# A byte offset for one operand of the combined column tiles

## The chip, the cores and the metric

The kernel runs on one core of one Trainium2 chip. The metric is the device time of one execution in microseconds. The kernel before takes 2104.44 us, the median of three runs (2104.36 to 2105.59).

## What is computed

One decoder block on a sequence of 512 tokens of width 2048, in float32. The part that matters here is the second half, the gated feed-forward:

```
h = rms_norm(x, norm2) * (1 + sc2) + sh2
gate, val = split(h @ w_up)            # w_up: 2048 x 12288
gate = causal_dwconv(gate, ffn_conv_w, ffn_conv_b)
x = x + g2 * ((gelu(gate) * val) @ w_down)
return rms_norm(x, norm_final)
```

Before it come the conditioning (`c` through `w_ada`), the input projection, two mixers and the output projection.

## The kernel before

Activations lie transposed, 128 features by 512 tokens to a tile. A float32 matrix product is made of products of rounded parts: a weight tile `raw` (128 x 1024) is rounded by ScalarE into `wh` (`round_up`, L163), and VectorE writes what was cut off, `raw - wh`, into `wl` (`rest`, L168), the weights' rest. Activations have such a pair too, `hi` and `lo`.

The program is a list of 516 steps, one weight tile each. A step has its tile rounded and its rest written two steps ahead (`round_step`, `rest_step` in the main loop), so that `wh` and `wl` have three buffers each, in a pool of their own at the low end of SBUF.

The stages are: 96 steps of input and output projections, 16 steps for the first four columns of `w_up` (`PLAIN`), 308 steps of combined columns, and 96 steps of `w_down`. Plain steps use `mm_w` or `mm_h`: per weight slice of 128 columns three matmuls of 512 columns, `wh` with `hi`, `wh` with `lo` and `wl` with `hi` (L174 to L176; `mm_h`, L181 to L183, has the roles of weights and activations exchanged).

A combined column is one of the other 44 columns of 128 gate and 128 value features. It is made of seven products of sums of weight blocks with sums of activation blocks (`P1` to `P7`, `product`), each one step. Such a step does eight times the same pair of matmuls:

```
PE.matmul(both, hi[:, cs], m, start=first, stop=False, skip_group_check=True)
PE.matmul(ps[:, lower], lo[:, cs], m[:, 0, :], start=False, stop=last, skip_group_check=True)
```

The first (L921) has 128 columns of `wh` as the stationary operand and 512 moving columns, the `hi` and `lo` parts of 256 tokens; the second (L922) has the same 128 columns of the rest `wl` and 256 moving columns. Each needs its own weight load. In these steps the weight tile is not fetched by `fetch` but named by `source[j]`: a tile `rawb`, `raw` or `t` that DMAs and VectorE have summed (`column`). `source` therefore holds just the 308 combined steps.

The order of instructions is the order in which the main loop issues them (`manual_schedule`); no planner moves them.

In the built program `wh` begins at bytes 1152, 5248 and 9344 of a partition and `wl` at 13440, 17536 and 21632. All matmul operands of the combined steps begin at a multiple of 64 bytes, and at the same remainder by 512.

Of the kernel before, what the change touches and what calls it, by code (L numbers as in the profile page):

```python
# [10 lines left out]
F32R = mybir.dt.float32r  # L11
# [4 lines left out]
P = 128  # L16
S = 512
# [14 lines left out]
NMM = 6  # L32
NXS = 24
WBUFS = 3


ROUNDS = [(0, 2), (2, 6), (6, 10), (10, 16)]
# [13 lines left out]
def tile_block(ctx, tc, x_t, vec, w_ada, w_in, w_r, w_i, ws_t, w_out, w_up, w_us, w_dn, out):  # L51
# [3 lines left out]
    wts = ctx.enter_context(tc.tile_pool(name="weights", bufs=1))  # L55
# [5 lines left out]
    def sb(tag, bufs, shape=(P, S), dt=F32, pl=pool):  # L61
        count[0] += 1
        return pl.tile(list(shape), dt, name=f"{tag}_{count[0]}", tag=tag, bufs=bufs)
# [97 lines left out]
    def round_up(raw):  # L161
        hi = sb("wh", WBUFS, (P, 2, S), F32R, wts)
        A.copy(hi, raw)  # L163
        return hi

    def rest(raw, hi):
        lo = sb("wl", WBUFS, (P, 2, S), F32R, wts)
        V.tensor_tensor(out=lo, in0=raw, in1=hi, op=SUB)  # L168
        return [(hi[:, kk, :], lo[:, kk, :]) for kk in range(2)]

# [90 lines left out]
    raws, his, ws, source = {}, {}, {}, {}  # L261
# [12 lines left out]

    def rest_step(j):
        if j < len(steps):
            ws[j] = rest(raws.pop(j), his.pop(j))

    def group(srcs, ks, op, rhs, done, small=0):

# [250 lines left out]
    round_step(0)  # L531
    next(cgen)
    rest_step(0)
    settle_h()
    round_step(1)
    fetch(3, SY)
    need(1)
    rest_step(1)
    fetch(4, SY)

# [623 lines left out]
    for f in range(FT):  # L1164
        if f < EARLY + 26:
            j = J1 + f // 2
# [6 lines left out]
    for k in range(KT):  # L1173
        j = place["P1", PLAIN + 2 + 5 * k // 2]
# [31 lines left out]
    for j, (_, go, done) in enumerate(steps):  # L1206
# [5 lines left out]
        if j == UP0:  # L1212
            rest_step(j + 1)
# [85 lines left out]
```

## Time and profile before

| what | value |
| --- | --- |
| median of three runs | 2104.44 us |
| profiled execution, device time | 2104.92 us |
| its span, first to last instruction | 2103.2 us |
| TensorE busy | 2069.0 us (98%) |
| VectorE busy | 1492.9 us (71%) |
| ScalarE busy | 923.8 us (44%) |
| combined columns, first to last matmul | 688.78 to 1559.26 us of the span |
| mean granted clock of TensorE | 0.993 of full speed |

The page gives the busy share of each engine, then the chain of work that ended last, then groups of instructions. A matmul's start is measured and its end is modelled, so that back-to-back matmuls overlap in the record; the distance from one start to the next tells what a matmul takes in a stream.

### The profile page before, as it was taken

The page shows a single profiled execution, that of the slowest core. Times are in us where ns is not written, and L with a number is a line of the kernel's source. Part 1 is how long each engine was busy: PE and PEld are TensorE (multiplying, and loading weights), DVE is VectorE, ACT ScalarE, POOL GpSimd, SP SyncE. Part 2 cuts the span into 40 slices and gives each one's busy share as a digit, 9 for nine tenths or more (in the row PEclk, how much of TensorE's full clock was granted, in tenths as well). Part 3 has the DMA queues.
Part 4 walks back from the last instruction along what each step waited for, and adds up shares of the span by engine and source line. Part 5 has one row for each costly group of instructions (what it writes and reads, how often), then busy time and mean ns, then how long its engine had stood idle before and what let it go on. Part 6 is the DMA issues. An engine that isn't in the chain of part 4 may idle for free.

```text
span 2103.2 us, 26309 instructions
## 1 busy us (share of the span) xinstructions
PE 2069.0 (98%) x10160; PEld 1727.6 (82%) x10160; DVE 1492.9 (71%) x1865; ACT 923.8 (44%) x1165; POOL 79.7 (4%) x100
## 2 busy tenths in 40 slices
PE   7999999999989999999999999999999999999997
PEld 4887777888868888888888888888888888888886
DVE  8999889788767888888888888888875223432333
ACT  5323666332234555555555555555553222322223
POOL 0000000000000000000000000000000000000000
PEclk9999999999999999999999999999999999999999
DMA  9977434589825677877877867767755334423222
GB/s 374 327 288 264 141 127 154 199 296 367 298 95 159 212 225 202 241 216 202 242 216 204 240 211 210 248 198 235 216 177 199 121 119 141 159 91 99 92 90 100
DMA packets 116061, 420.36 MB, mean 200 GB/s; under 512 B 14816, under 2 KB 14944, under 8 KB 103648
## 3 DMA queue, kind: packets, MB, share of 16 engines
q1 hardware_dynamic: 87280, 315.39, 42.6%
q0 software_dynamic: 12672, 46.14, 11.6%
q10 hardware_dynamic: 15984, 57.15, 7.9%
q8 instruction: 80, 1.31, 0.2%
q14 instruction: 45, 0.37, 0.0%
HBM read 397.66 MB, written 20.97 MB: 199 GB/s over the span
## 4 chain that ended last, share of the span: by engine, by line
PE 87%; DVE 7%; ACT 3%; issue 1%; DMA 1%; SPq 0%; ACTq 0%; DVEq 0%
PE mm L921 28%; PE mm L922 14%; PE mm L174 13%; PE mm L175 13%; PE mm L176 13%; DVE araw L212 2%; PE mm L181 1%; PE mm L183 1%; PE mm L182 1%; DVE wl L168 1%; DMA araw<-w_ada 1%; DVE xs L359 1%; PE sm L655 0%; DVE la L685 0%; DVE xs L734 0%
## 5 line engine op out<-in xcount | busy, mean ns | idle before, releaser
L163 ACT CAST wh<-raw 128x1024 fp32r<-128x1024 f32 x296 | 311.7, 1053 | 615.1 <-PE mm L175 443.1
L168 DVE TENSOR_TENSOR wl<-raw,wh 128x1024 fp32r<-128x1024 f32 x296 | 360.9, 1219 | 303.8 <-ACT wh L163 303.4
L921 PE MATMUL mm<-hp,wh 128*128 128x512 f32 x1408 | 499.5, 399 | 0.0
L174 PE MATMUL mm<-hp,wh 128*128 128x512 f32 x1184 | 469.0, 396 | 6.7 <-ACT hp L229 5.8
L175 PE MATMUL mm<-hp,wh 128*128 128x512 f32 x1184 | 463.6, 392 | 0.5 <-DVE hp L237 0.5
L176 PE MATMUL mm<-hp,wl 128*128 128x512 f32 x1184 | 462.8, 391 | 0.0
L922 PE MATMUL mm<-hp,wl 128*128 128x256 f32 x1408 | 395.4, 281 | 0.0
L921 PE MATMUL mm<-xs,wh 128*128 128x512 f32 x1056 | 375.1, 399 | 0.0
L921 PEld LDWEIGHTS mm<-hp,wh 128*128 128x128 f32 x1408 | 264.6, 188 | 66.1
L922 PE MATMUL mm<-xs,wl 128*128 128x256 f32 x1056 | 296.6, 281 | 0.0
L174 PEld LDWEIGHTS mm<-hp,wh 128*128 128x128 f32 x1184 | 223.7, 189 | 58.3 <-ACT hp L229 8.7
L922 PEld LDWEIGHTS mm<-hp,wl 128*128 128x128 f32 x1408 | 266.0, 189 | 0.0
L175 PEld LDWEIGHTS mm<-hp,wh 128*128 128x128 f32 x1184 | 223.6, 189 | 50.1 <-issue 2.4
L176 PEld LDWEIGHTS mm<-hp,wl 128*128 128x128 f32 x1184 | 223.6, 189 | 46.6
L168 DVE TENSOR_TENSOR wl<-rawb,wh 128x1024 fp32r<-128x1024 f32 x176 | 214.9, 1221 | 65.6 <-ACT wh L163 65.6
L921 PEld LDWEIGHTS mm<-xs,wh 128*128 128x128 f32 x1056 | 198.4, 188 | 49.6
L922 PEld LDWEIGHTS mm<-xs,wl 128*128 128x128 f32 x1056 | 199.5, 189 | 0.0
L163 ACT CAST wh<-rawb 128x1024 fp32r<-128x1024 f32 x176 | 185.2, 1052 | 23.9 <-PE mm L921 13.3
L212 DVE SCALAR_TENSOR_TENSOR araw<-araw,crow 128x2050 f32<-128x2050 f32 (+1 forms) x80 | 182.6, 2286 | 2.5 <-DMA araw<-w_ada 2.4
L950 POOL DMA_DIRECT2D raw<-w_us x88 | 75.9, 862 | 1240.8 <-DMA rawb<-w_us 457.8
L974 ACT COPY u<-mm 128x512 f32<-128x512 f32 x88 | 51.7, 587 | 161.5 <-PE mm L922 161.5
L168 DVE TENSOR_TENSOR wl<-t,wh 128x1024 fp32r<-128x1024 f32 x44 | 53.9, 1225 | 50.3 <-ACT wh L163 50.3
(233 smaller groups left out, 2106.3 us busy)
## 6 DMA issues: line engine op xcount, KB each, us to landing
rawb<-w_us SPq DMA_DIRECT2D x132, 512.0 KB, 6.8
araw<-w_ada SPq DMA_DIRECT2D x48, 1024.5 KB, 7.6
raw<-w_dn SPq DMA_DIRECT2D x96, 512.0 KB, 3.6
raw<-w_us SPq DMA_DIRECT2D x88, 512.0 KB, 6.2
raw<-w_us POOLq DMA_DIRECT2D x88, 512.0 KB, 7.3
araw<-w_ada SPq DMA_DIRECT2D x32, 1025.0 KB, 8.4
raw<-w_in ACTq DMA_DIRECT2D x59, 512.0 KB, 4.6
yl<-w_ada SPq DMA_DIRECT2D x16, 1024.5 KB, 5.4
```

The source lines that it names most:

```text
L163: A.copy(hi, raw)
L168: V.tensor_tensor(out=lo, in0=raw, in1=hi, op=SUB)
L174: PE.matmul(ps, w[0][:, cs], h[0], start=first, stop=False)
L175: PE.matmul(ps, w[0][:, cs], h[1], start=False, stop=False)
L176: return PE.matmul(ps, w[1][:, cs], h[0], start=False, stop=last)
L181: PE.matmul(ps, h[0][:, cs], w[0], start=first, stop=False)
L182: PE.matmul(ps, h[0][:, cs], w[1], start=False, stop=False)
L212: V.scalar_tensor_tensor(out=raw, in0=raw, scalar=1.0, in1=crow[:, :w], op0=MUL, op1=MUL, accum_out=mods[:, n:n + 1])
L921: PE.matmul(both, hi[:, cs], m, start=first, stop=False, skip_group_check=True)
L922: PE.matmul(ps[:, lower], lo[:, cs], m[:, 0, :], start=False, stop=last, skip_group_check=True)
L950: G.dma_start(o[name], w_us[f - PLAIN, i], accum_op=ADD)
L974: A.copy(t, o["x"])
```

## The change

`wl` buffers grow from 1024 to 1088 float32 per partition, 4096 to 4352 bytes. In the 308 combined steps the rest is written to, and read from, elements 8 to 1031 of its buffer, in all other steps from elements 0 to 1023.

```diff
+OFFSET = 8
...
-    def rest(raw, hi):
-        lo = sb("wl", WBUFS, (P, 2, S), F32R, wts)
+    def rest(raw, hi, off=0):
+        whole = sb("wl", WBUFS, (P, 2 * S + 64), F32R, wts)
+        lo = whole[:, off:off + 2 * S].rearrange("p (a b) -> p a b", a=2)
         V.tensor_tensor(out=lo, in0=raw, in1=hi, op=SUB)
...
-            ws[j] = rest(raws.pop(j), his.pop(j))
+            ws[j] = rest(raws.pop(j), his.pop(j), OFFSET if j in source else 0)
```

On all five engines the instructions, their order and their waits are row for row the same. What differs is where tiles lie: `wl` begins at bytes 13440, 17792 and 22144, and 32 more in the combined steps, and what stands above it in the lower part of SBUF (`yl`, `fy`, `rawb`, `dp`, `t2`, `gw`, `vw` and others) moves up by 768 bytes. `wh`, `hp`, `xs` and `raw` stay.

## Rows read from the trace of the kernel before

**Rows 1.** Page, part 1 (busy us, share, instructions) and part 4 (chain, by engine).

```profile
PE 2069.0 (98%) x10160; PEld 1727.6 (82%) x10160; DVE 1492.9 (71%) x1865; ACT 923.8 (44%) x1165; POOL 79.7 (4%) x100
...
PE 87%; DVE 7%; ACT 3%; issue 1%; DMA 1%; SPq 0%; ACTq 0%; DVEq 0%
```

**Rows 2.** Busy time in one stretch of the combined columns, with granted clock.

```profile
core 0: us, PE busy (x) PEld busy (x) DVE busy (x) ACT busy (x) POOL busy (x), PEclk, DMA share, GB/s
700.00:1569.60 869.60, 869.60 (x4911) 753.60 (x4910) 720.27 (x781) 477.84 (x575) 72.29 (x84) 1.00 0.74 219
```

**Rows 3.** Page, part 5: the second matmul of a pair, by moving tile.

```profile
L922 PE MATMUL mm<-hp,wl 128*128 128x256 f32 x1408 | 395.4, 281 | 0.0
...
L922 PE MATMUL mm<-xs,wl 128*128 128x256 f32 x1056 | 296.6, 281 | 0.0
```

**Rows 4.** Timeline, TensorE, into the combined columns: start us, modelled length, instruction.

```profile
688.55 0.39 PE L176 MATMUL mm<-hp,wl 128*128 128x512 f32 x1
688.78 0.39 PE L921 MATMUL mm<-hp,wh 128*128 128x512 f32 x1
689.00 0.28 PE L922 MATMUL mm<-hp,wl 128*128 128x256 f32 x1
689.12 0.40 PE L921 MATMUL mm<-hp,wh 128*128 128x512 f32 x1
689.35 0.28 PE L922 MATMUL mm<-hp,wl 128*128 128x256 f32 x1
689.47 0.40 PE L921 MATMUL mm<-hp,wh 128*128 128x512 f32 x1
689.71 0.28 PE L922 MATMUL mm<-hp,wl 128*128 128x256 f32 x1
689.83 0.40 PE L921 MATMUL mm<-hp,wh 128*128 128x512 f32 x1
```

**Rows 5.** Timeline, TensorE, out of the combined columns into `w_down`.

```profile
1559.26 0.28 PE L922 MATMUL mm<-hp,wl 128*128 128x256 f32 x1
1559.38 0.40 PE L174 MATMUL mm<-xs,wh 128*128 128x512 f32 x1
...
1560.31 0.39 PE L175 MATMUL mm<-xs,wh 128*128 128x512 f32 x1
```

**Rows 6.** Timeline, TensorE, in `w_down`: eleven plain matmuls, first and last.

```profile
1619.69 0.39 PE L176 MATMUL mm<-dp,wl 128*128 128x512 f32 x1
...
1621.96 0.39 PE L174 MATMUL mm<-dp,wh 128*128 128x512 f32 x1
```

**Rows 7.** Timeline, matmuls (PE) and weight loads (PEld) of one pair.

```profile
1200.04 0.40 PE L921 MATMUL mm<-hp,wh 128*128 128x512 f32 x1
1200.04 0.19 PEld L922 LDWEIGHTS mm<-hp,wl 128*128 128x128 f32 x1
...
1200.27 0.28 PE L922 MATMUL mm<-hp,wl 128*128 128x256 f32 x1
1200.27 0.19 PEld L921 LDWEIGHTS mm<-hp,wh 128*128 128x128 f32 x1
```

**Rows 8.** Weight loads elsewhere: a timeline row, then two lines' min/median/max ns.

```profile
592.56 0.97 PEld L136 LDWEIGHTS sm<-ones,sqs 128*128 128x128 f32 x8 [2.72 <-issue]
...
L515 PEld LDWEIGHTS sm<-xs,ones x16: 186/190/191, 10.3 to 17.4; 128*128 128x128 f32 x16
...
L655 PEld LDWEIGHTS sm<-la,wi x16: 186/190/190, 203.3 to 317.8; 128*128 128x128 f32 x16
```

**Rows 9.** VectorE's writes: duration min/median/max ns, first and last start.

```profile
L168 DVE TENSOR_TENSOR wl<-rawb,wh x176: 1210/1220/1226, 679.0 to 1554.2; 128x1024 fp32r<-128x1024 f32 x176
...
L212 DVE SCALAR_TENSOR_TENSOR araw<-araw,crow x80: 2262/2286/2296, 18.5 to 570.9; 128x2049 f32<-128x2049 f32 x48, 128x2050 f32<-128x2050 f32 x32
```

## The prediction

> **What bounds the kernel.** The page comes first. TensorE is busy for 98% of the span and holds 87% of the chain of work that ended last [rows 1]. Then comes the stage that the change touches, the combined columns. [...]
>
> The number of pairs is the count of L922, 1408 with a moving tile `hp` and 1056 with `xs`, in sum 2464 [rows 3]. The pitch comes from the timeline: the first L921 starts at 688.78 [rows 4], the last L922 at 1559.26 [rows 5]. That is 870.48 us for 2463 whole pairs and one step from L921 to L922 (0.24), so 870.24 / 2463 = 0.3533 us a pair. The reader should see how even this is: in [rows 4] the pairs after the first begin at 689.12, 689.47 and 689.83, so 0.35 and 0.36 apart, and the stage as a whole has the same mean.
>
> Is 0.3533 all that the matmuls need? Two rows say that it is a little more. In a plain stream of 512-column matmuls, each with a weight load of its own, ten steps take 1621.96 - 1619.69 = 2.27 us, 0.227 each [rows 6]. The first pair of the stage, which comes after such a stream, takes 689.12 - 688.78 = 0.34: 0.22 to 0.23 for the 512 columns and 0.11 to 0.12 for the 256. From the second pair on the 512-column step takes 0.23 to 0.24 [rows 4]. And when the stage ends, four 512-column matmuls in `w_down` take 1560.31 - 1559.38 = 0.93, 0.2325 each, before that stream runs at 0.227 too [rows 5, 6]. So in the pairs something costs 0.3533 - 0.34 = 0.0133 us each, and it needs some matmuls to die away. What differs from a plain stream is that weight loads come more densely: one begins with every matmul [rows 7], and a matmul of 256 columns is over in 0.12 while eight loads behind one another, with matmuls of one column, take 0.97 us, some (0.97 - 0.19) / 7 = 0.111 each [rows 8]. Loads nearly fill the short matmul and reach into the long one. That much the rows bear out; whether the disturbance has to do with the byte at which an operand begins they don't show, since before the change all operands of the pair begin at the same remainder by 512 bytes.
>
> **The change part by part.** It removes and adds no instruction, moves none and adds no wait. Four things remain to be costed.
>
> First, the 2464 loads of a rest, which now begin 32 bytes past a multiple of 64. This is the term on which all hangs, and no row shows it directly. The nearest is a load of `ones`, a tile that lies 32 bytes past a multiple of 64 in the kernel before: L515 loads it 16 times, in 186 to 191 ns, and L655 loads gate weights, which begin at a multiple of 64, in 186 to 190 ns [rows 8]. The load itself thus takes the same. These matmuls are unrounded float32 ones, though, in which the load has much more room, so that the row bounds the load and not a conflict of the load with the stream beside it. From both sides: at best the disturbance is gone and every pair takes the 0.34 of the first, 2464 x -0.0133 = -32.8 us; at worst every pair takes the 0.36 that now one in three shows, 2464 x (0.36 - 0.3533) = +16.5 us. I take 0, by [rows 8], for a second reason too: the load of a rest runs beside the long matmul, 0.23 us [rows 7] for a load that alone needs 0.111. The load in the tight place, beside the 256 columns, is that of `wh`, and `wh` isn't moved.
>
> [...]
>
> Second, the 308 writes of a rest by VectorE at the new start. Now a write takes 1220 ns [rows 9]. The nearest row is L212, which works in place on two buffers of 8200 bytes, 8224 apart: every other one begins 32 bytes past a multiple of 64. All 80 take 2262 to 2296 ns [rows 9], with no second level among them. So 0, and a cover stands behind it: VectorE is idle for 869.60 - 720.27 = 149.3 us of the stage [rows 2], 0.49 us for each of some 307 writes, so that a write must become 40% longer before VectorE is what the stage waits for. A rest is written two steps, 16 pairs, ahead of its use in the program's order.
>
> Third, the 208 plain rests, two thirds of them in buffers that begin 256 or 512 bytes further on. Their stream takes 0.227 with moving tiles that lie in quite different places, `hp`, `xs` and `dp` among them, so 0.
>
> Fourth, the tiles above that move by 768 bytes. That is a multiple of 64 and of 256, none of them is a weight, and only `dp` is a moving operand. 0.
>
> The sum is 0 against the profiled 2104.92 us, of which 2103.2 are the span and 1.7 lie around it. The median of the runs is 0.5 lower, and I forecast that median: 2104.4.
>
> **The rivals.** *Faster: the shift parts the load of the rest from the stream beside it.* If the disturbance comes from load and stream reading at the same remainder of an address, the shift takes the rest's half of it away. Then the long step goes back to the 0.227 of a plain stream and the short one stays at the 0.12 of [rows 4]: 0.347 a pair, 2464 x (0.347 - 0.3533) = -15.5 us, 2088.9. For it speaks that the excess is there and lies in the long step, in which the rest is loaded. Against it: that step may be long only because the load of `wh`, begun beside the 256 columns, isn't done when it starts, and this one keeps its place. A whole recovery, 2071.6, would need both.
>
> *Slower: the shift puts the load of the rest in the stream's way.* The place is the same step, from L921 to L922. If a start that isn't a multiple of 64 costs the load an extra read, or moves it into the slots of the 512 moving columns, each pair goes to the slow 0.36: +16.5 us, 2120.9. A load that only takes longer decides nothing until it exceeds 0.227, twice its 0.111; one that takes slots from the stream costs from the first pair on. Against it stands the equal load of `ones`.
>
> *The change doesn't do what it says.* Only steps in `source` get the offset, and these are all 308 products, each with one write and eight loads; the built program has the offset on all of them. No chance is kept for this.
>
> **How the numbers follow.** Nothing changes: 0.60. Faster by the recovery: 0.22, since the excess is in the rows and depends on how loads and streams meet. Slower by a new conflict: 0.18, since with equal ignorance of addresses the shift may do harm as well as good, but has less room by the row of `ones`. A partial effect is as likely as a full one, so that the two prices are spread from the edge of "the same" to their ends. A measurement tells 0.2% from no change here, 4.2 us. The range takes in no change, recoveries down to 2090 and losses up to 2114, some three fifths of the price; it leaves out about 0.15. The chances are 0.22 faster, 0.60 within 0.2%, 0.18 slower.
>
> **What would show it.** If I am right, the pair's pitch in the combined columns is 0.3533 after as before, with the same steps of 0.23 to 0.24 and 0.12, the stage lasts 870.5 us, writes of the rest stay at 1220 ns and TensorE is still busy for the whole of it. The faster rival shows as a long step of 0.227 and a stage of some 855 us; the slower one as a pair of 0.36 and some 887 us. A write of the rest well above 1.22 us with TensorE waiting for it would break the second step; a plain stream off 0.227 would break the third or the fourth.

## The result and the profile after

The changed kernel takes 2089.44 us, the median of four runs (2087.23 to 2090.37), against 2104.89 us before, the median of four runs on the same occasion. The ratio is 0.9923, with a 95% interval from 0.9911 to 0.9936: 15.5 us faster, where no change was forecast.

The profiled execution took 2090.37 us with a span of 2088.6 us, 14.6 us less than before. Page, part 1, which answers to [rows 1]:

```profile
PE 2053.3 (98%) x10160; PEld 1720.6 (82%) x10160; DVE 1493.7 (72%) x1865; ACT 919.8 (44%) x1165; POOL 81.3 (4%) x100
```

TensorE's busy time fell by 15.7 us with the same 10160 matmuls; VectorE's rose by 0.8. Timeline of TensorE, from the first pair of the combined columns to the last, with eight steps out of the middle (start us, modelled length, instruction); L924 and L925 are the lines that were L921 and L922:

```profile
690.14 0.40 PE L924 MATMUL mm<-hp,wh 128*128 128x512 f32 x1
...
1200.44 0.40 PE L924 MATMUL mm<-xs,wh 128*128 128x512 f32 x1
1200.68 0.28 PE L925 MATMUL mm<-xs,wl 128*128 128x256 f32 x1
1200.80 0.39 PE L924 MATMUL mm<-xs,wh 128*128 128x512 f32 x1
1201.02 0.28 PE L925 MATMUL mm<-xs,wl 128*128 128x256 f32 x1
1201.13 0.40 PE L924 MATMUL mm<-xs,wh 128*128 128x512 f32 x1
1201.37 0.28 PE L925 MATMUL mm<-xs,wl 128*128 128x256 f32 x1
1201.49 0.39 PE L924 MATMUL mm<-xs,wh 128*128 128x512 f32 x1
1201.71 0.28 PE L925 MATMUL mm<-xs,wl 128*128 128x256 f32 x1
...
1544.22 0.28 PE L925 MATMUL mm<-hp,wl 128*128 128x256 f32 x1
```

The stage lasts 1544.22 - 690.14 = 854.08 us instead of 870.48 [rows 4, 5]. That is 16.40 us less; the stage began 1.36 us later than before and what follows it took 0.44 longer, which together give the span's 14.6. A pair now takes (854.08 - 0.23) / 2463 = 0.3467 us instead of 0.3533. The eight steps show how: every second pair is a fast one of 0.22 + 0.11 (1200.80 to 1201.13), the one behind it takes 0.24 + 0.12. In the trace the two pitches are 340 and 353 to 354 ns in turn, from the sixth pair to the end of the stage; the first five take 349 to 352. Before, the 340 stood only at the very start [rows 4]; from there on the pairs took 350, 361 and 349 ns in turn, a cycle of three.

Busy time in nearly all of the stage, which answers to [rows 2]: TensorE still never waits (844.00 us busy of 844.00, before 869.60 of 869.60), and its granted clock is 1.00 as before.

```profile
700.00:1544.00 844.00, 844.00 (x4872) 739.09 (x4871) 712.86 (x771) 468.22 (x569) 72.29 (x84) 1.00 0.75 222
```

VectorE's write of the rest (L171, before L168) and a plain stream of eleven matmuls in `w_down`, which answer to [rows 9] and [rows 6]:

```profile
L171 DVE TENSOR_TENSOR wl<-rawb,wh x176: 1210/1220/1228, 680.4 to 1539.4; 128x1024 fp32r<-128x1024 f32 x176
```

```profile
1605.79 0.39 PE L178 MATMUL mm<-dp,wh 128*128 128x512 f32 x1
...
1608.05 0.39 PE L179 MATMUL mm<-dp,wl 128*128 128x512 f32 x1
```

The write takes 1220 ns as before, and ten plain steps take 2.26 us, 0.226 each, as before. So all of the gain is the pitch of the pair.

### The profile page after: what moved, and what is told of

Read it like the earlier page. It is cut to its first block, busy times and chain, and to the rows that moved or that the text cites. A ratio compares the mean times of both kernels' runs of the same rounds, so it can differ in the third digit from the quotient of the medians.

```text
span 2088.6 us, 26309 instructions
## 1 busy us (share of the span) xinstructions
PE 2053.3 (98%) x10160; PEld 1720.6 (82%) x10160; DVE 1493.7 (72%) x1865; ACT 919.8 (44%) x1165; POOL 81.3 (4%) x100
## 4 chain that ended last, share of the span: by engine, by line
PE 87%; DVE 7%; ACT 3%; issue 1%; DMA 1%; SPq 0%; ACTq 0%; DVEq 0%
PE mm L924 27%; PE mm L925 14%; PE mm L177 13%; PE mm L178 13%; PE mm L179 13%; DVE araw L215 2%; PE mm L184 1%; PE mm L186 1%; PE mm L185 1%; DVE wl L171 1%; DMA araw<-w_ada 1%; DVE xs L362 1%; PE sm L658 0%; DVE la L688 0%; DVE xs L737 0%
## 5 line engine op out<-in xcount | busy, mean ns | idle before, releaser
L171 DVE TENSOR_TENSOR wl<-raw,wh 128x1024 fp32r<-128x1024 f32 x296 | 362.0, 1223 | 303.9 <-ACT wh L165 303.5
L924 PE MATMUL mm<-hp,wh 128*128 128x512 f32 x1408 | 490.3, 394 | 0.0
L925 PE MATMUL mm<-hp,wl 128*128 128x256 f32 x1408 | 391.3, 278 | 0.0
L924 PE MATMUL mm<-xs,wh 128*128 128x512 f32 x1056 | 368.2, 394 | 0.0
L924 PEld LDWEIGHTS mm<-hp,wh 128*128 128x128 f32 x1408 | 264.2, 188 | 60.7
L925 PE MATMUL mm<-xs,wl 128*128 128x256 f32 x1056 | 293.4, 278 | 0.0
L925 PEld LDWEIGHTS mm<-hp,wl 128*128 128x128 f32 x1408 | 264.4, 188 | 0.0
L171 DVE TENSOR_TENSOR wl<-rawb,wh 128x1024 fp32r<-128x1024 f32 x176 | 215.0, 1221 | 57.9 <-ACT wh L165 57.9
L924 PEld LDWEIGHTS mm<-xs,wh 128*128 128x128 f32 x1056 | 198.1, 188 | 45.5
L925 PEld LDWEIGHTS mm<-xs,wl 128*128 128x128 f32 x1056 | 198.3, 188 | 0.0
L171 DVE TENSOR_TENSOR wl<-t,wh 128x1024 fp32r<-128x1024 f32 x44 | 53.9, 1225 | 50.5 <-ACT wh L165 50.5
```

## The experiments

What the runs had to tell apart: whether the 32 bytes did it or the new places of the longer buffers; whether a start of its own counts (within 64 bytes) or a distance between two operands; if a distance, that of a load from the moving stream or of the two loads from each other; and whether the distance is all that counts.

All pitches below are from one start of the first matmul of a pair to the next. Where they are given in ns, they are worked out from the starts in the trace; in the table they are means over the last 50 pairs of a block of seven steps. A time without an interval is that of one run. Edits are against the changed kernel, but for the three kernels that shift activations, which start from the kernel before.

### The longer buffers without the 32 bytes

```diff
-OFFSET = 8
+def offsets(j):
+    return 0, 0
...
-            ws[j] = rest(raws.pop(j), his.pop(j), OFFSET if j in source else 0)
+            ws[j] = rest(raws.pop(j), his.pop(j), offsets(j)[1])
```

> The longer rest buffers stay, the 32 bytes go: every rest starts at the beginning of its buffer. If the 32 bytes are the cause, the pitch of a pair in the combined columns is back at 0.3533 us and the time at 2104.9 us. If it is the new places of the buffers (256 and 512 bytes further on) or of the tiles above them, the pitch stays at 0.3467 us and the time at 2089.4 us.

2104.43 us against 2104.24, ratio 1.0004 (0.9995 to 1.0014). First matmuls of a pair in 700 us of the combined columns (busy us of TensorE, count in brackets), before and here:

```profile
800.00:1500.00 700.00, 700.00 (x1982) 372.29 (x1982) 1.00 0.75 222
```

```profile
800.00:1500.00 700.00, 700.00 (x1982) 372.26 (x1982) 1.00 0.75 222
```

In the changed kernel the same 700 us hold 2021:

```profile
800.00:1500.00 700.00, 700.00 (x2021) 378.90 (x2020) 1.00 0.76 224
```

So it is the 32 bytes. That two of the three buffers begin 256 and 512 bytes further on, and the tiles above 768, did nothing.

### Sweeps of the start

Two kernels give each block of seven combined steps an offset of its own.

```diff
+LIST = (0, 1, 2, 3, 4, 5, 6, 7, 8, 10, 12, 14, 16, 18, 20, 24, 28, 32, 40, 48, 56, 64)
...
-            ws[j] = rest(raws.pop(j), his.pop(j), OFFSET if j in source else 0)
+            ws[j] = rest(raws.pop(j), his.pop(j), offsets(j)[1])
```

> The start of the rest differs by combined column: 0, 1, 2, 3, 4, 5, 6, 7, 8, 10, 12, 14, 16, 18, 20, 24, 28, 32, 40, 48, 56, 64 elements (4 bytes each), seven steps with each, and all of them once more; in the last 96 steps four steps with each. If what counts is that the start is not a multiple of 64 bytes (16 elements), pairs take 0.3467 us at every offset but 0, 16, 32, 48 and 64. [...] If it is the distance between two streams, the pitch rises and falls smoothly with the offset, and with no return at 16. Plain matmuls in the last steps stay at 0.227 us at every offset if their loads are hidden.

> The same 22 offsets, given in the first 22 combined columns to the rounded weights alone, the rests at 0; in the other 22 to both alike. Theory one, a load conflicts with the moving stream beside it when both start at the same remainder: shifting both frees both loads, so that the pitch at 8 elements is at most 0.3467 us, perhaps 0.340. Theory two, the two loads that follow one another get in each other's way when they start at the same remainder: shifting the rounded weights alone by 8 gives 0.3467 us as shifting the rests does, and shifting both alike brings 0.3533 us back.

The second kernel has `round_up` take `offsets(j)[0]` in the same way. Each of the two took 2105.84 us. Some of the pitches, in ns, by offset in elements of 4 bytes:

| offset | rest alone, first and second pass | `wh` alone | both alike |
| --- | --- | --- | --- |
| 0 | 353.2, 346.7 | 353.2 | 346.7 |
| 1 | 346.7, 346.7 | 346.6 | 350.0 |
| 2 | 351.1, 351.1 | 346.6 | 346.7 |
| 3 | 356.7, 356.7 | 353.2 | 349.9 |
| 4 | 353.3, 353.3 | 350.0 | 346.7 |
| 8 | 346.7, 346.7 | 351.2 | 353.3 |
| 12 | 346.7, 346.7 | 349.3 | 346.7 |
| 16 | 346.7, 346.7 | 340.0 | 353.3 |
| 24 | 351.7, 351.7 | 350.0 | 346.7 |
| 56 | 353.3, 353.3 | 346.7 | 346.7 |
| 64 | 346.7, 346.7 | 346.7 | 353.2 |

No expectation held as a whole. The pitch isn't a matter of multiples of 64 bytes (4 and 56, which are none, take 353.3; 16 and 64, which are, take 346.7), and it doesn't rise and fall smoothly (346.7 at 1, 356.7 at 3, 346.7 again at 8, 351.7 at 24). Theory one fails as it was stated, since shifting both by 8 is no better than shifting none. Theory two had one thing right, the 353.3 with both shifted by 8, but fails: `wh` alone by 8 doesn't give what the rest alone gives, and with both alike the distance between the two loads stays while the pitch still changes, to 350.0 at 1 and 349.9 at 3. What the table does show: a move of a single element can change the pitch (351.1 at 2, 356.7 at 3 and 353.3 at 4, rest alone, in both passes); all offsets but 0 give the same in both passes, while 0 gives two values; and one entry, `wh` alone by 16 elements, stands at 340.0. In the sweep each entry of the last two columns was met once, behind the offset before it, so that it holds for that way of entering alone.

Plain matmuls weren't indifferent either. In `w_down`, with four steps to an offset of the rest, they took 227.1 ns at 0 and 226.7 at 7, but 229 to 234 at the other offsets short of 64, and 227.5 at 64 (256 bytes). `wh` shifted alone by less than 64 gave 230 to 234. For plain streams the starts of the kernel before are about the best of those tried.

### The activations shifted, by padding

```diff
-        return sb("hp", 16, (P, 2, S), dt)
+        whole = sb("hp", 16, (P, 2 * S + 16), dt)
+        return whole[:, 8:8 + 2 * S].rearrange("p (a b) -> p a b", a=2)
```

> The kernel before, but the pairs of activations (hp) start 32 bytes further on; weights stay. Of the seven products of a column, those with hp as the moving tile then have load and stream at different remainders, those with xs as before. Theory one (load against stream): the pairs with hp take 0.3467 us or less, those with xs 0.3533 us. Theory two (load against load): 0.3533 us everywhere.

2114.8 us. The padding of 64 bytes did more than the expectation says: from one of the 16 buffers to the next 64 bytes more are added up, so that they stand at four different distances from the weights by the remainder of 256 bytes. Plain matmuls with `hp` took 234 ns, pairs with `hp` 349.3 and with `xs`, which weren't moved, 346.8. That the latter changed too says that one pair acts on later ones, so that the comparison within the run doesn't tell the two theories apart; the 346.8 at starts that didn't move is close to the second pitch, 346.7, that offset 0 has in the table. The two runs that follow shift all buffers alike.

### All operands shifted, and the stream alone

A tile of 32 bytes at the low end of the weights' pool, and one at the high end of the main pool, move whole pools.

```diff
     wts = ctx.enter_context(tc.tile_pool(name="weights", bufs=1))
+    wts.tile([P, 8], F32, name="ahead")
...
+    pool.tile([P, 56], F32, name="behind")
     own.__exit__(None, None, None)
```

> Weights, rests and activations all lie 32 bytes further on by the remainder of 256, so that every distance between two operands of a pair stays and only their own remainders change. If distances count, a plain matmul takes 0.227 us and a pair 0.3533 us, 2104.9 us in all. If an operand's own start within 64 bytes counts, plain matmuls take 0.231 us or more, as in the sweep with the weights alone off, and the time rises by some 20 to 30 us.

2106.22 us, one run beside 2104.42. The count in the same 700 us:

```profile
800.00:1500.00 700.00, 700.00 (x1982) 372.23 (x1982) 1.00 0.75 221
```

Every block has 353.2 to 353.4 ns, and plain matmuls with `hp` take 0.227, six in 1.36 us:

```profile
1649.77 0.39 PE L175 MATMUL mm<-hp,wh 128*128 128x512 f32 x1
...
1651.13 0.39 PE L175 MATMUL mm<-hp,wh 128*128 128x512 f32 x1
```

With all distances kept, nothing changes, though not one operand of a pair begins at a multiple of 64 bytes any more. So a start as such doesn't count, at least for a move of 32 bytes, and what is left is the distance.

The second kernel has only the tile behind, of 32 bytes, which moves `hp` and `xs` down and leaves weights, rests and `dp`:

```diff
+    pool.tile([P, 8], F32, name="behind")
     own.__exit__(None, None, None)
```

> The moving tiles hp, xs and all others of the upper pool lie 32 bytes further down, weights and rests stay. If the distance between a load and the moving stream counts, this is what shifting both loads by 8 elements is: a pair takes 0.3533 us and a plain matmul of hp with weights more than 0.227 us. If only the distance between the two loads counts, nothing changes: 0.3533 us, 0.227 us, 2104.9 us.

2128.79 us, 24 us slower than 2104.42, as the first half of the expectation has it. Timeline of TensorE, two pairs in the combined columns, then six plain steps in `w_down` with `hp` and six with `dp`:

```profile
999.70 0.40 PE L921 MATMUL mm<-hp,wh 128*128 128x512 f32 x1
999.94 0.28 PE L922 MATMUL mm<-hp,wl 128*128 128x256 f32 x1
1000.06 0.39 PE L921 MATMUL mm<-hp,wh 128*128 128x512 f32 x1
1000.29 0.28 PE L922 MATMUL mm<-hp,wl 128*128 128x256 f32 x1
1000.41 0.40 PE L921 MATMUL mm<-hp,wh 128*128 128x512 f32 x1
...
1650.54 0.40 PE L174 MATMUL mm<-hp,wh 128*128 128x512 f32 x1
...
1651.94 0.40 PE L174 MATMUL mm<-hp,wh 128*128 128x512 f32 x1
...
1699.90 0.39 PE L176 MATMUL mm<-dp,wl 128*128 128x512 f32 x1
...
1701.26 0.39 PE L176 MATMUL mm<-dp,wl 128*128 128x512 f32 x1
```

Six plain steps with `hp` take 1.40 us, 0.233 each instead of 0.227, and so they do through the run with `hp` and `xs`; with `dp`, which didn't move, six take 1.36, still 0.227. The distance between the two kinds of load is the same here as before, so it is the distance of a load from the moving stream that costs the plain steps their 6 ns. The pairs take 0.3533 us as both loads shifted by 8 do in the table, and by the same two-pair cycle, 361 and 346 ns in turn: 0.24 + 0.12, then 0.23 + 0.12. The kernel before has the same mean by its cycle of three, so that an equal mean doesn't say that nothing changed.

### The same starts with two pitches

The table's first row has two values for the same starts. This kernel has the starts of the kernel before in all but the first seven combined steps.

```diff
+def offsets(j):
+    return 0, 56 if 112 <= j < 119 else 0
```

> The rest starts 56 elements further on in the first seven combined steps, and at 0 in the other 301, as in the kernel before. If the starts alone decide the pitch, these 301 take 0.3533 us a pair, and the time is 2104.9 us. In the sweep the second column with offset 0, which came after 56 and 64, took 0.3467 us, so that the same starts seem to have two steady pitches, and the one found on entering stays: then the 301 steps take 0.3467 us and the time is 2089 us.

2090.08 us against 2104.42, as the second half of the expectation has it. Timeline of TensorE where the offset ends (the start at 709.72 is the first with starts as before):

```profile
709.01 0.39 PE L927 MATMUL mm<-hp,wh 128*128 128x512 f32 x1
709.24 0.28 PE L928 MATMUL mm<-hp,wl 128*128 128x256 f32 x1
709.36 0.40 PE L927 MATMUL mm<-hp,wh 128*128 128x512 f32 x1
709.59 0.28 PE L928 MATMUL mm<-hp,wl 128*128 128x256 f32 x1
709.72 0.39 PE L927 MATMUL mm<-hp,wh 128*128 128x512 f32 x1
709.94 0.28 PE L928 MATMUL mm<-hp,wl 128*128 128x256 f32 x1
710.06 0.39 PE L927 MATMUL mm<-hp,wh 128*128 128x512 f32 x1
710.29 0.28 PE L928 MATMUL mm<-hp,wl 128*128 128x256 f32 x1
710.41 0.39 PE L927 MATMUL mm<-hp,wh 128*128 128x512 f32 x1
```

The first block runs at 353.3 ns and all 43 others at 346.7, with every pair alike at 0.23 + 0.12: 2408 pairs whose operands all begin at the same remainder by 256 bytes as before the change, and which are 6.7 ns faster each. The starts of the kernel before thus have two steady pitches, and which of them holds is decided by the matmuls that lead into them. The mean is that of the changed kernel, but the cycle isn't: there the pairs take 340 and 353 in turn.

A second kernel enters with `wh` shifted by 16 in the first seven steps:

```diff
+def offsets(j):
+    return (16, 0) if 112 <= j < 119 else (0, 0)
```

> The rounded weights start 16 elements further on in the first seven combined steps, and at 0 in the other 301, where all starts are those of the kernel before. If a steady pitch once entered stays, the 301 steps keep the 0.3400 us of the first seven, and the time is 2072 us. If the starts of the kernel before only allow 0.3467 and 0.3533 us, they take one of these: 2088 or 2104 us.

2104.96 us, so the old pitch came back. The first block has 340.0 ns, and with its end the slow cycle is back (the fast pair from 708.24 is the last):

```profile
707.90 0.39 PE L928 MATMUL mm<-hp,wh 128*128 128x512 f32 x1
708.12 0.28 PE L929 MATMUL mm<-hp,wl 128*128 128x256 f32 x1
708.24 0.39 PE L928 MATMUL mm<-hp,wh 128*128 128x512 f32 x1
708.47 0.28 PE L929 MATMUL mm<-hp,wl 128*128 128x256 f32 x1
708.58 0.40 PE L928 MATMUL mm<-hp,wh 128*128 128x512 f32 x1
708.81 0.28 PE L929 MATMUL mm<-hp,wl 128*128 128x256 f32 x1
708.93 0.40 PE L928 MATMUL mm<-hp,wh 128*128 128x512 f32 x1
```

So 0.340 didn't hold at the old starts in this run: the stream before doesn't carry it over, the distance has to stay.

### The offset in every step

```diff
-OFFSET = 8
+def offsets(j):
+    return 0, 8
...
-            ws[j] = rest(raws.pop(j), his.pop(j), OFFSET if j in source else 0)
+            ws[j] = rest(raws.pop(j), his.pop(j), offsets(j)[1])
```

> The rest starts 32 bytes further on in all 516 steps, not in the 308 combined ones alone. The combined columns should stay at 0.3467 us a pair. The plain steps of the sweep with this start took 0.2332 us a matmul instead of 0.227: 4992 plain matmuls x 0.0064 = +32 us on the 2089.4 of the changed kernel at most, some 2115 to 2121 us, as the first stage waits for other engines too. If only dense loads, as in the pairs, were open to the distance, the plain ones would stay at 0.227 us, and the time at 2089.4 us.

2114.78 us, against 2103.50 for the kernel before and just short of the 2115 to 2121 that were expected. The combined columns stay at 0.3467. Plain steps in `w_down`:

```profile
1619.83 0.40 PE L180 MATMUL mm<-dp,wh 128*128 128x512 f32 x1
...
1621.93 0.40 PE L180 MATMUL mm<-dp,wh 128*128 128x512 f32 x1
```

Nine steps in 2.10 us, 0.233 each. Over the plain steps this loses some 25 us against the changed kernel's 2089.44, more than the combined columns gain: the condition on `source` is what makes the change pay.

### The rounded weights shifted by 64 bytes

```diff
+def offsets(j):
+    return (16, 0) if 112 <= j < 420 else (0, 0)
```

> In the combined steps the rounded weights start 16 elements (64 bytes) further on and the rests at 0; all other steps at 0. The column of the sweep that had these starts took 0.3400 us a pair, the two steps 0.227 and 0.113. If the starts decide, the whole stage runs so: 2464 x 0.340 = 837.8 us instead of 870.5, and the time is 2071.8 us. If how the stream came into that column decided it, the stage stays above 0.340, at 0.3467 us a pair and 2088 us.

2072.03 us against 2104.42, ratio 0.9843 (0.9826 to 0.9859): twice the gain of the change, with intervals that don't touch. Timeline of TensorE from the first pair on, and the last matmul of the stage:

```profile
689.99 0.40 PE L928 MATMUL mm<-hp,wh 128*128 128x512 f32 x1
690.22 0.28 PE L929 MATMUL mm<-hp,wl 128*128 128x256 f32 x1
690.34 0.39 PE L928 MATMUL mm<-hp,wh 128*128 128x512 f32 x1
690.57 0.28 PE L929 MATMUL mm<-hp,wl 128*128 128x256 f32 x1
690.68 0.39 PE L928 MATMUL mm<-hp,wh 128*128 128x512 f32 x1
690.91 0.28 PE L929 MATMUL mm<-hp,wl 128*128 128x256 f32 x1
691.02 0.39 PE L928 MATMUL mm<-hp,wh 128*128 128x512 f32 x1
...
1527.64 0.28 PE L929 MATMUL mm<-hp,wl 128*128 128x256 f32 x1
```

From the second pair on all take 0.34, in every block, and the stage lasts 1527.64 - 689.99 = 837.65 us. The buffers of `wh` had to grow here as those of the rest did. That isn't the cause: the kernel that shifts `wh` in the first seven steps alone has the same buffers, and its other 43 blocks run at 353. At 0.340 nothing is lost against a plain stream: 768 columns at 0.2267 us for 512 are 0.340. This pitch was reached by two ways of entering, from plain steps here and from another offset in the sweep.

## Why the prediction was wrong

**What bounds the kernel** was right. TensorE waits for nothing in the combined columns (it is busy for all of 869.60 us before [rows 2] and of 844.00 after, at a granted clock of 1.00), and the time moved by the pair's pitch times 2464: 2464 x (0.3467 - 0.3533) = -16.3 us, measured -16.4.

**The excess of 0.0133 us a pair** was read rightly, as something that weight loads and the stream beside them do to each other and that takes a few matmuls to die away: behind the stage before, four plain matmuls take 0.2325 us each and then 0.227 [rows 5, 6]. All of it can be had back, as the kernel at 2072.03 us shows. The dense loads that the prediction named as what differs aren't enough to cause it, though: at 0.340 us a pair the loads come more densely still and nothing is lost, and plain steps, with sparser loads, lose 6 ns each, 0.233 us for 0.227, with the stream alone 32 bytes further down.

**The first term, the loads of the rests, was the step that failed.** It was set at 0 and measures -16.4 us. Two reasons carried the 0, and neither bore it. The load of `ones` [rows 8] was taken as the nearest row because its tile, too, lies 32 bytes past a multiple of 64, although the prediction itself says that this row bounds the load and not a conflict with the stream beside it. But what counts isn't a start, as the run with all operands shifted shows, and the length of a load's record tells nothing of the stream beside it: the record of the rest's load has a mean of 189 ns before and 188 after. The other reason was that the rest's load runs beside the long matmul and has room there. The rows of the changed kernel speak against it: that load was moved, and both steps became shorter, from 0.2363 and 0.1170 us on average to 0.2317 and 0.1150. The cycles of two pairs (340 and 353 ns) and of three (350, 361 and 349) show that a disturbance runs on from pair to pair, so it can't be costed load by load.

**The second to fourth terms** were right: writes of 1220 ns, plain steps of 0.227, tiles above without effect.

**The faster rival** had the right price, 2088.9 us against 2089.44, and in part the wrong mechanism, so that the price is luck in part. Its sign was a long step of 0.227 in every pair with the short one at 0.12; measured is a long step of 0.227 in every second pair alone, and a mean of 0.2317 and 0.1150. It put the excess down to load and stream reading at the same remainder. But at the same remainders the pairs can also run at 0.3467, so that an equal remainder doesn't force the 0.3533; what the change ended is a slow cycle into which the old starts happen to fall on entering from a plain stream. A whole recovery was said to need both loads moved. It came with `wh` alone moved, by 64 bytes, and with both moved alike none of the offsets tried brought it.

**The slower rival** didn't come here, but shifts that cost time exist: the same 32 bytes cost the plain steps 0.006 us each, and three elements in place of eight gave 356.7 ns a pair in the sweep.

The chance for the forecast, 0.60, rested on one row of the wrong kind. The rows did show the excess, its two ends and that nothing bore on the dependence on addresses; with that, the three outcomes should have been held about even, and the range have reached to the rival's 2088.9.

**What stays open.** Whether load and stream share a resource, and which, isn't shown, nor why the old starts have two pitches and which event on entering chooses. That the distance of load and stream counts is shown for plain steps, and for pairs by the cycle that changes when the stream alone is moved and by the table's last column; a part of the two loads' distance from each other isn't ruled out in the pairs. Nor is it shown why the commonest values lie 6.7 ns apart, 340.0, 346.7 and 353.3 for a pair and 226.7 and 233.3 for a plain step. Whether 0.340 is the floor of a pair, and 0.227 that of a plain step, wasn't tried beyond the offsets named.

## What to carry to other kernels

Where TensorE is the bound, compare the pitch of a dense stream with that of the same matmuls where loads are sparser, or with the first of the stage; an excess of a few per cent with no wait in it can be a matter of where stationary and moving operands lie relative to each other, as it was here, 0.3533 us a pair against 0.340. Then sweep the distance, one offset to a block of steps in a single run, and read the pitch of each block: it costs one run and no instruction, and no reasoning from alignments found the best offset here. Apply it only to the stage where it pays, confirm it over the whole stage, since a pitch can depend on how the stream was entered (353.3 or 346.7 ns here), and look again whenever a pool's size changes: 32 bytes more in the main pool cost 24 us here.

## What the runs showed of the hardware

- In these runs the start-to-start time of matmuls that never waited changed with the distance in bytes between weight loads and moving operand: 340.0 to 356.7 ns for the same pair, 227 to 234 for the same plain matmul. Moving everything alike by 32 bytes changed nothing (353.3 and 227 ns), and two of the rest's three buffers 256 and 512 bytes further on changed nothing either (1982 pairs in 700 us, as before).
- A single element of 4 bytes was enough: for the rest alone 346.7 ns a pair at 1, 351.1 at 2, 356.7 at 3, 353.3 at 4, the same in both passes.
- The same starts held two steady pitches, 353.3 and 346.7 ns, each for more than 2400 pairs without a break, depending on the matmuls that led into them.
